# Loading and starting the next slab's norm one input block earlier, with its instructions ranked above others

## The chip, the cores and the metric

The kernel runs on one core of one Trainium2 chip. The metric is the device time of one execution in microseconds (us); lower is better. The core has a matrix engine (PE, with its weight loads as a row of their own, PEld), three engines for elementwise work (DVE, ACT, POOL), and SP, which here only issues transfers. Each engine works through its own instructions in the order in which they were written, and waits at each for the semaphores that it needs.

## The reference, cut to what matters

One inference step of a two-layer encoder, on a prompt of 2048 frames and 32 sample frames, each 1024 wide. Layer 0 mixes by sliding-window attention, layer 1 by a gated delta rule. Each layer starts with an RMS norm of its whole input; that norm is what the change moves.

```python
def rmsnorm(x, g):
    y = x * lax.rsqrt(jnp.mean(x * x, axis=-1, keepdims=True) + EPS) * g
    return y

for i in range(DEPTH):                       # DEPTH = 2
    hp = rmsnorm(xp, norm_g[i])              # prompt
    hs = rmsnorm(xs, norm_g[i])              # sample
    if i % N_MIXERS == 0:
        yp, kp, vp = attn_prompt(hp, ...)    # (softmax attention * silu(gate)) @ w_out
        ys, kd, vd = attn_sample(hs, ...)
    else:
        yp, cp, sp = deltanet_branch(hp, ...)  # conv, delta rule in chunks of 64, norm, gate, @ w_out
        ys, cd, sd = deltanet_branch(hs, ...)
    xp = xp + yp
    xs = xs + ys
y_prompt = rmsnorm(xp, final_norm_g)
y_sample = rmsnorm(xs, final_norm_g)
```

## The kernel before, in words

**Slabs and blocks.** The frames are cut into four slabs of 512 columns; slab 1 also carries the 32 sample frames and is 544 wide, worked as two groups of 272. Features lie on the 128 partitions, so a slab's input is eight tiles (k = 0 to 7). A layer's input projection goes block by block, 128 output features each: 20 input blocks a slab in the attention layer (weights `wa`), 33 in the delta layer (`wd`), then eight output blocks (`wao`, `wdo`). Every float32 operand is split into a high and a low part, and a block is 8 x 3 matmuls into the PSUM tile `pj`: 24 matmuls of 512 columns, or 48 of 272 in slab 1. The matmuls read the normalised input from tiles called `hk` (high and low part side by side) and the weights from `wh`.

**One slab's norm.** `normed` makes three steps. `start` gets the row scales and spreads them over all partitions into the tile `rb`. `ahead` loads the first three of the eight input tiles into `xa`, a ring of three buffers. `pre` starts `norm`, which for each k multiplies `xa` by `rb` and the norm's weight (DVE, scalar_tensor_tensor), casts the result into the high half of an `hk` tile (ACT), subtracts to get the low half (POOL in the attention layer, DVE in the delta layer: the argument `gcol` decides), and then loads tile k + 3 into the buffer that this frees. The input comes from `in_x` in the attention layer and from a scratch tensor (shown as `xsx`) in the delta layer.

**Buffers.** `hk` is a ring of 16. It holds a slab's eight normalised tiles and the eight tiles of the mixer's output (`og`, shown as `hk<-of` in attention and `hk<-zs` in the delta layer), which the output blocks read. A new `hk` tile takes the buffer of the one made 16 tiles earlier and can be written only when that one has been read for the last time.

**When a norm starts.** `run_blocks` walks the blocks. As a block begins it chooses the next one and calls that one's `ahead`; the block's own `pre` is called before its first matmul. The first input block of a slab carries its norm's `ahead` and `pre`. So the loads of slab n + 1 are written when slab n's last input block begins, and its norm when its own first block begins. The last input block of a slab (attention slabs, and delta slabs but the last) is marked `beside`: its matmuls are ranked as if they stood beside the block before it, so the two run interleaved. The delta layer's first slab is set apart: its norm is started from output block 2 of the last attention slab.

**Order.** Beside the blocks run generators ("sides"): the attention of a head pair, the chunks of the delta rule, the norms. They are advanced while the blocks are written down, by an estimated clock of PE. Nothing goes straight to an engine: each operation is put on a list with its dependencies and a rank,

```python
self.rank += 1
op.rank = (self.rank - self.lead, self.rank)
```

and at the end of a layer `Order.flush` plays the list through with estimated costs. Whenever an engine is free it takes, of the operations that are then ready, the one of the lowest rank. The result is the fixed order of that engine's instructions on the chip. `lead` is normally 0; evacuations of `pj` get `EVAC` = 400 and the delta rule's chain of states `CHAIN` = 600. `step`, which resumes a side, sets `lead` to 0 first. One input block at the end of a slab is some 75 to 230 operations. Some operations run far ahead of their rank, because their engine has nothing better to do.

**Which block comes next.** `pick` takes an output block of slab n if the mixer of slab n has ended on the estimated clock, and otherwise the next input block of slab n + 1 (in attention at most its first six before slab n's output blocks have all been written).

The functions that the change touches, and what calls them:

## Time and profile before

| | |
|---|---|
| three runs | 2372.67, 2376.36, 2381.98 us (median 2376.36) |
| profiled execution | 2376.4 us, its span 2374.6 us |
| mean granted TensorE clock | 0.978 |
| PE busy | 2252.8 us, 95% of the span |
| PEld, DVE, ACT, POOL busy | 1843.9, 1639.6, 1262.2, 862.9 us |
| matmuls into `pj` | 1770.1 us of PE |
| HBM traffic | 311.63 MB read, 68.19 MB written |

All instructions of this kernel carry the line of one helper (L185), so the profile is read by tile names: `pj<-hk,wh` is a projection's matmul, `xa<-xa,par,rb` the norm's multiplication, `hk<-xa` its cast, `hk<-xa,hk` its subtraction. `<-` in square brackets names what ended the idle time before an instruction. In a timeline the first number is the start in us from the beginning of the span and the second the duration.

### The profile page before, as it was taken

Reading aid. Unit: us, or ns where it says so; the run is one execution under the profiler, and the core shown is the slowest. Engines: PE = TensorE matmul, PEld = TensorE weight load, DVE = VectorE, ACT = ScalarE, POOL = GpSimd, SP = SyncE. Lnnn points to the kernel's source line nnn. Section 1 sums busy time; section 2 is a strip of 40 time slices with the busy share of each in tenths; the row PEclk is TensorE's granted clock in tenths of the full one; section 3 lists DMA queues with packets and bytes.
Section 4 is the critical chain, followed back from the end, with each engine's and each line's share of the span. In section 5 each row is a group of like instructions: output and inputs, shape, how many; then the busy total and the mean of one; then the engine's idle time right before and its main releaser. Section 6 shows DMA issues by size and latency. Waiting matters only on the chain.

```text
span 2374.6 us, 44457 instructions
## 1 busy us (share of the span) xinstructions
PE 2252.8 (95%) x14759; PEld 1843.9 (78%) x14759; DVE 1639.6 (69%) x5024; ACT 1262.2 (53%) x3792; POOL 862.9 (36%) x1044
## 2 busy tenths in 40 slices
PE   8998999999999999999999999989999999999997
PEld 5777788797778777777778788877798767777776
DVE  6765465626553445588887768889786888876876
ACT  5555466636553554455566354564644466445533
POOL 4556555665554334222322121331312222122222
PEclk9998999999999999999999999999999999999998
DMA  7556755585434115544423664333456634466442
GB/s 253 175 187 192 255 188 181 174 279 190 147 105 150 62 63 159 193 149 140 143 89 126 200 227 136 128 115 122 147 172 215 200 118 138 134 215 216 155 142 67
DMA packets 222832, 382.75 MB, mean 161 GB/s; under 512 B 29922, under 2 KB 45194, under 8 KB 222602
## 3 DMA queue, kind: packets, MB, share of 16 engines
q1 hardware_dynamic: 220154, 377.75, 49.4%
q8 instruction: 116, 1.90, 0.3%
q10 hardware_dynamic: 2448, 2.16, 0.3%
q14 instruction: 114, 0.93, 0.1%
HBM read 311.63 MB, written 68.19 MB: 160 GB/s over the span
## 4 chain that ended last, share of the span: by engine, by line
PE 56%; DVE 28%; ACT 7%; issue 4%; DMA 3%; POOL 2%; SPq 0%; DVEq 0%; ACTq 0%; POOLq 0%
PE pj L185 39%; PE tb L185 6%; PE ta L185 5%; PE tc L185 4%; DVE cy L185 4%; DVE s L185 3%; DVE sub L185 3%; DVE tl L185 3%; ACT s L185 2%; DVE ml L185 2%; ACT ta L185 1%; DVE xa L185 1%; DVE r L185 1%; DVE md L185 1%; DVE mx L185 1%
## 5 line engine op out<-in xcount | busy, mean ns | idle before, releaser
L185 PE MATMUL pj<-hk,wh 128*128 128x512 f32 (+1 forms) x8184 | 1770.1, 364 | 26.9 <-DVE xr L185 8.6
L185 PEld LDWEIGHTS pj<-hk,wh 128*128 128x128 f32 x8184 | 1326.6, 191 | 237.9 <-issue 14.1
L185 POOL TENSOR_TENSOR wh<-wr,wh 128x512 fp32r<-128x512 f32 x224 | 295.5, 1321 | 328.2 <-ACT wh L185 283.7
L185 DVE SCALAR_TENSOR_TENSOR cy<-cx,cw,cy 128x512 f32<-128x512 f32 x360 | 230.6, 651 | 44.7 <-ACT cy L185 41.1
L185 ACT CAST wh<-wr 128x512 fp32r<-128x512 f32 x224 | 138.1, 618 | 203.6 <-PE pj L185 157.3
L185 ACT ACTIVATE s<-s,mx 128x256 f32<-128x256 f32 (+1 forms) x272 | 132.0, 487 | 30.1 <-DVE mx L185 29.9
L185 ACT ACTIVATE qs<-tb,egq 64x128 f32<-64x128 f32 x264 | 95.7, 362 | 89.7 <-DVE r L185 76.5
L185 DVE TENSOR_TENSOR sub<-ml,tl 128x60 f32<-128x60 f32 (+24 forms) x527 | 125.8, 239 | 10.2
L185 DVE TENSOR_SCALAR s<-s,den 128x256 f32<-128x256 f32 (+1 forms) x272 | 130.9, 530 | 1.2
L185 ACT ACTIVATE cx<-cy 128x512 f32<-128x512 f32 (+1 forms) x96 | 61.1, 636 | 130.9 <-DVE cy L185 101.5
L185 DVE TENSOR_TENSOR tl<-tl,sub 128x60 f32<-128x60 f32 (+24 forms) x527 | 122.3, 232 | 10.1
L185 DVE CUSTOM_DVE_ANT_0 s<-ta,bias 128x256 f32<-128x256 f32 (+1 forms) x272 | 95.7, 405 | 43.5 <-PE ta L185 42.9
L185 POOL TENSOR_TENSOR pr<-pr,ph 128x512 fp32r<-128x512 f32 x82 | 111.8, 1364 | 34.9 <-ACT ph L185 28.8
L185 POOL COPY cx<-hist 128x3 f32<-128x3 f32 x96 | 25.5, 265 | 263.9 <-DVE kq L185 63.6
L185 DVE TENSOR_TENSOR xr<-pj,xr 128x512 f32<-128x512 f32 (+1 forms) x72 | 41.2, 577 | 112.1 <-PE pj L185 70.1
L185 POOL TENSOR_TENSOR so<-so,mhalf 128x4 f32<-128x4 f32 x33 | 36.8, 1115 | 216.9 <-DVE so L185 189.1
L185 DVE SCALAR_TENSOR_TENSOR r<-tb,nbk,vb 64x128 f32<-64x128 f32 x264 | 91.7, 348 | 29.6 <-PE tb L185 25.1
L185 ACT ACTIVATE qs<-o 128x128 f32<-128x128 f32 x132 | 40.7, 308 | 133.8 <-DVE o L185 128.3
L185 ACT COPY cx<-pj 128x512 f32<-128x512 f32 (+2 forms) x149 | 64.1, 445 | 77.5 <-PE pj L185 62.1
L185 PE MATMUL tb<-st,kq 128*128 128x128 f32 x512 | 94.7, 286 | 6.8 <-DVE st L185 5.9
L185 PEld LDWEIGHTS tb<-st,kq 128*128 128x128 f32 x512 | 82.9, 194 | 21.5 <-DVE st L185 13.0
L185 PE MATMUL tb<-con,s 128*128 128x128 f32 (+2 forms) x528 | 77.7, 280 | 18.9 <-DVE s L185 16.0
(242 smaller groups left out, 3558.0 us busy)
## 6 DMA issues: line engine op xcount, KB each, us to landing
wh<-xswwd SPq DMA_DIRECT2D x528, 256.0 KB
wr<-in_wa SPq DMA_DIRECT2D x160, 256.0 KB
wh<-xswwdo SPq DMA_DIRECT2D x112, 256.0 KB
pr<-in_wd SPq DMA_DIRECT2D x66, 256.0 KB
xswwd<-ph SPq DMA_DIRECT2D x66, 256.0 KB
xswwd<-pr SPq DMA_DIRECT2D x66, 256.0 KB
wr<-in_wao SPq DMA_DIRECT2D x64, 256.0 KB
xa<-in_x SPq DMA_DIRECT2D x48, 256.0 KB
```

The costliest lines, as they stand in the source:

```text
L185: self.order.add(Op(self.name, lambda: call(*args, **kw), cost, op == "dma_start"), ins, outs)
```

## The change

Two edits. In `run`, for each slab but the last of each layer, the next slab's `ahead` is called after the third last input block (index -3) and its `pre` after the second last (index -2), and both hooks are taken off the next slab's first block. So the loads and the norm's operations are each written one input block earlier, the norm's during the slab's last input block. In `norm`, `lead` is set to `EVAC` ahead of each piece of its work, so every multiplication, cast, subtraction and load of tiles 3 to 7 has a rank lower by 400. The first three loads, written by `ahead`, keep lead 0. The norm of the delta layer's first slab is called from where it was, but has the new rank too. The operations themselves, their number and shapes stay the same.

```diff
             for k in range(KT + 1):
+                self.issue.lead = Order.EVAC
                 if k < KT:
                     nc.vector.scalar_tensor_tensor(
                         out=o.x[k], in0=o.x[k], scalar=self.par[:, gcol + k : gcol + k + 1], in1=o.rb[:, :n], op0=ALU.mult, op1=ALU.mult)
                 if k:
                     yield o.x[k - 1]
                     h = self.t(self.hp, [P, 2, 544], "hk", F32R, bufs=16)
+                    self.issue.lead = Order.EVAC
                     nc.scalar.copy(h[:, 0, :n], o.x[k - 1])
                     yield
+                    self.issue.lead = Order.EVAC
                     self.low(o.x[k - 1], h[:, 0, :n], h[:, 1, :n], nc.vector if gcol else nc.gpsimd)
                     o.h.append(h)
                     if k + 2 < KT:
                         o.x.append(self.load_x(src, k + 2, slab, "xa", 3))
+                self.issue.lead = 0
...
                 out[-1].post = lambda si=si, stat=stat: (self.made.add(f"oa{si}"), self.spawn(stat(), "rstd", 1000))
+                if si + 1 < ns:
+                    self.then(blocks[-3], h1[si + 1].ahead)
+                    self.then(blocks[-2], h1[si + 1].pre)
+                    h1[si + 1].ahead = h1[si + 1].pre = None
...
                     out = self.last_outs(si, slab, og, over)
+                if si + 1 < ns:
+                    self.then(blocks[-3], h2[si + 1].ahead)
+                    self.then(blocks[-2], h2[si + 1].pre)
+                    h2[si + 1].ahead = h2[si + 1].pre = None
```

## The prediction

> **What bounds the kernel now.** I read the page's spans first, then PE's busy time in the seven stretches where one slab ends and the next begins, then PE's waits, then the timeline of two such stretches.

> ```profile
> span 2374.6 us, 44457 instructions
> PE 2252.8 (95%) x14759; PEld 1843.9 (78%) x14759; DVE 1639.6 (69%) x5024; ACT 1262.2 (53%) x3792; POOL 862.9 (36%) x1044
> ```

> PE is the bound: it is idle for 2374.6 - 2252.8 = 121.8 us in all, and no reordering can win more than that unless the clock changes. The windows show where a norm could matter (stretch, length, then busy us of PE, PEld, DVE, ACT and POOL with their instructions, then granted clock, DMA share and GB/s):

> ```profile
> 170.00:212.00 42.00, 33.65 (x201) 26.60 (x199) 33.35 (x73) 24.08 (x67) 26.36 (x22) 0.76 0.53 165
> 440.00:472.00 32.00, 27.71 (x205) 20.29 (x203) 23.42 (x65) 22.15 (x66) 24.62 (x24) 1.00 0.57 186
> 670.00:700.00 30.00, 26.26 (x182) 20.22 (x181) 22.89 (x60) 19.46 (x54) 17.03 (x16) 1.00 0.32 92
> 890.00:914.00 24.00, 21.62 (x160) 16.14 (x156) 21.33 (x56) 16.25 (x43) 9.69 (x9) 1.00 0.37 110
> 1200.00:1232.00 32.00, 28.90 (x232) 24.22 (x231) 24.23 (x87) 24.00 (x95) 12.26 (x19) 0.95 0.19 58
> 1570.00:1610.00 40.00, 31.39 (x201) 23.44 (x200) 34.44 (x111) 21.29 (x68) 15.77 (x24) 0.91 0.39 117
> 1930.00:1956.00 26.00, 22.77 (x139) 17.81 (x137) 24.44 (x66) 16.33 (x55) 11.43 (x14) 0.93 0.36 108
> sum 226.00, PE 192.32 PEld 148.72 DVE 184.10 ACT 143.56 POOL 117.16; mean PE 27.47 PEld 21.25 DVE 26.30 ACT 20.51 POOL 16.74
> ```

> The first three are the attention slabs' boundaries (call them A1, A2, A3), the fourth the step into the delta layer (X), the last three the delta slabs' (D1, D2, D3). Length minus PE busy gives idle times of 8.35, 4.29, 3.74, 2.38, 3.10, 8.61 and 3.23 us: 226.00 - 192.32 = 33.7 us, 1.4% of the span. That is what the change can reach. Only part of it is put down to the norm by name:

> ```profile
> PE tc L185 <- ACT pt L185: 6.9, 5, 4.7
> ...
> PE ta L185 <- DVE tq L185: 4.9, 9, 1.8
> PE pj L185 <- ACT hk L185: 4.8, 5, 2.1
> ...
> PE pj L185 <- DVE hk L185: 3.9, 3, 2.2
> ...
> PE pj L185 <- DMA wh<-xswwd: 3.0, 5, 0.7
> ```

> Projections wait for the norm's cast and subtraction (hk) for 4.8 + 3.9 = 8.7 us. The rest of the 33.7 are holes in the mixer's own chain, as the 4.7 us on a softmax copy (pt), which a projection that was ready could have filled.

> **The change part by part.** Nothing is added or removed. Moved are, per norm, the rows of this view:

> ```profile
> L185 DVE SCALAR_TENSOR_TENSOR xa<-xa,par,rb x80: 714/752/1920, 177.2 to 2177.1; 128x512 f32<-128x512 f32 x56, 128x544 f32<-128x544 f32 x24
> L185 SPq DMA_DIRECT2D xa<-in_x x64: 327/333/1462, 25.0 to 680.3; - x64
> L185 ACT CAST hk<-xa x56: 601/620/657, 178.0 to 1952.5; 128x512 fp32r<-128x512 f32 x40, 128x544 fp32r<-128x544 f32 x16
> ...
> L185 DVE TENSOR_TENSOR hk<-xa,hk x32: 665/684/726, 902.4 to 1953.2; 128x512 fp32r<-128x512 f32 x24, 128x544 fp32r<-128x544 f32 x8
> ...
> L185 POOL TENSOR_TENSOR hk<-xa,hk x24: 1257/1304/1837, 178.7 to 689.8; 128x512 fp32r<-128x512 f32 x16, 128x544 fp32r<-128x544 f32 x8
> ```

> Eight multiplications (8 x 0.752 = 6.0 us of DVE), eight casts (8 x 0.620 = 5.0 us of ACT), eight subtractions (10.4 us of POOL in attention, 5.5 us of DVE in the delta layer) and the loads (0.33 us of SP each, twice as many in slab 1). All of it lies beside PE's work; what reaches PE is only when the last `hk` tile is there.

> How early can that be? Writing the norm one block earlier does not by itself let it start earlier: the first three multiplications wait only for `rb` and their loads and run long ahead of their rank where DVE is free, and the first cast waits for an `hk` buffer that the last input block frees. What can shrink is the time from the first cast to the last subtraction. D2 shows it:

> ```profile
> 1575.43 1.66 ACT L185 CAST hk<-xa 128x512 fp32r<-128x512 f32 x3
> ...
> 1582.19 0.69 DVE L185 TENSOR_TENSOR hk<-xa,hk 128x512 fp32r<-128x512 f32 x1
> ...
> 1582.93 0.96 PE L185 MATMUL pj<-hk,wh 128*128 128x512 f32 x3 [1.47 <-DVE hk L185]
> ...
> 1592.23 0.51 PE L185 MATMUL pj<-hk,wh 128*128 128x512 f32 x1 [1.28 <-ACT hk L185]
> ...
> 1595.59 4.15 PE L185 MATMUL pj<-hk,wh 128*128 128x512 f32 x10 [2.19 <-DVE hk L185]
> ...
> 1605.58 0.69 DVE L185 TENSOR_TENSOR hk<-xa,hk 128x512 fp32r<-128x512 f32 x1
> 1605.60 2.80 PE L185 MATMUL pj<-hk,wh 128*128 128x512 f32 x6 [2.08 <-ACT hk L185]
> ```

> Three casts are done by 1577.1, but the first subtraction comes at 1582.2, behind the delta rule's own work on DVE; only it frees a buffer for the fourth load. In A2 a free subtraction and what follows it look like this:

> ```profile
> 442.77 1.27 POOL L185 TENSOR_TENSOR hk<-xa,hk 128x512 fp32r<-128x512 f32 x1 [2.15 <-PE tb L185]
> ...
> 446.89 1.40 DVE L185 SCALAR_TENSOR_TENSOR xa<-xa,par,rb 128x512 f32<-128x512 f32 x1 [1.54 <-DMA xa<-in_x]
> ```

> From the subtraction's end (444.04) to the next multiplication are 2.85 us. With that a round of the three buffers takes 0.69 + 2.85 + 0.75 + 0.62 = 4.9 us, and three rounds end at 1576 + 15 = 1591 instead of 1606.3. So in D2 the rank can take the norm's end forward by up to 15 us, and with it the four named waits, 1.47 + 1.28 + 2.19 + 2.08 = 7.0 us. I take **-6** (bounds 0, if DVE's other work then ends late, and -8.61, all idle). In D1 the idle time is not put down to `hk`, and half its tiles have buffers long before: **-1** of 3.10 (bounds 0 and -3.10). D3 is like D2 with a smaller hole: **-2** of 3.23 (0 and -3.23).

> In attention the norm is not alone at the end of the boundary. A1:

> ```profile
> 178.72 3.11 POOL L185 TENSOR_TENSOR hk<-xa,hk 128x544 fp32r<-128x544 f32 x2 [2.98 <-ACT hk L185]
> 178.72 1.92 DVE L185 SCALAR_TENSOR_TENSOR xa<-xa,par,rb 128x544 f32<-128x544 f32 x1
> ...
> 184.27 1.60 PE L185 MATMUL tc<-pt,vt 128*64 128x128 f32 x12 [4.68 <-ACT pt L185]
> ...
> 187.97 0.64 ACT L185 CAST hk<-xa 128x544 fp32r<-128x544 f32 x1
> ...
> 208.68 1.34 POOL L185 TENSOR_TENSOR hk<-xa,hk 128x544 fp32r<-128x544 f32 x1
> ...
> 211.28 0.73 POOL L185 TENSOR_TENSOR hk<-of,hk 128x256 fp32r<-128x256 f32 x1 [1.26 <-ACT hk L185]
> 212.54 6.72 PE L185 MATMUL pj<-hk,wh 128*128 128x272 f32 x50 [0.91 <-DVE kl L185]
> ```

> The norm ends at 210.0, the slab's attention output at 212.0. The output blocks need the latter, so they cannot start before 212; but slab 1's second block (48 of the 50 matmuls at 212.54, 6.72 x 48/50 = 6.5 us) stands behind the norm and could run before 212 if the norm ended at 200. PE has room for it: 8.35 us idle. I take **-6** (bounds 0 and -8.35). The third multiplication, done at 180.6, has its cast only at 187.97: such gaps are what the rank closes.

> In A2 and A3 both first blocks are already done when attention ends:

> ```profile
> 470.71 1.08 POOL L185 TENSOR_TENSOR hk<-of,hk 128x256 fp32r<-128x256 f32 x2
> ...
> 472.13 0.52 PE L185 MATMUL pj<-hk,wh 128*128 128x272 f32 x2 [0.25 <-DVE kl L185]
> ```

> A norm that ends sooner only moves PE's hole, unless `pick`, which then meets the first blocks earlier on its clock with the attention still running, puts a third or fourth input block ahead of the output blocks. I take half the idle times, **-2** each (bounds 0 and -4.29, -3.74).

> X has only the new rank, and there it can hurt. The output blocks wait for attention's last piece, and the norm's DVE work now goes ahead of it:

> ```profile
> 910.68 0.74 POOL L185 TENSOR_TENSOR hk<-of,hk 128x256 fp32r<-128x256 f32 x1 [2.01 <-ACT hk L185]
> ...
> 914.46 2.45 DVE L185 SCALAR_TENSOR_TENSOR xa<-xa,par,rb 128x512 f32<-128x512 f32 x2
> ```

> Two multiplications and some three subtractions run after that piece now; if all pass it, it comes 2 x 0.75 + 3 x 0.68 = 3.6 us later. I take **+2** (bounds -2.38 and +3.6).

> Queues moved past: on POOL eight subtractions of 1.30 us pass weight splits, on SP five loads pass weight loads; if the load's buffer is late on the chip, what stands behind it waits up to a round trip, 2.85 us. I cost both at nothing, since weights are loaded a block ahead (a block is 24 matmuls, some 6 us) and PE waits only 3.0 us for them in the whole span; without that cover it is up to 2.85 us at each of six boundaries, +17.

> Sum: -6 - 2 - 2 + 2 - 1 - 6 - 2 = -17. The profiled execution took 2376.4 us (1.8 beyond its span), and the median of the runs shown is 2376.36, so **2376.4 - 17 = 2359.4, say 2360 us**. A change under 0.5% (11.9 us: below 2364.5 or above 2388.3) can hardly be told from none.

> **The rivals.** *Larger gain by the clock, 2347 us.* A1 has a granted clock of 0.76, where the other attention boundaries have 1.00. If its holes close and the clock stays up, the 33.65 us of busy time shrink by up to 0.24 x 33.65 = 8 us; with all idle of A1 and D2 gone as well (another 2.35 + 2.61 = 5) it is 2360 - 13. Against it: two attention chains still alternate on a DVE that is busy for 33.35 of 42 us. [...]

> *No change, about 2371.* The mixer's chain, not the norm, ends each boundary. Then A2 and A3 give nothing, A1 and D2 some 4 and 3, X costs 2: 2376.4 - 5. For it: PE's largest waits by name are the mixer's. Against it: the four waits in D2 are the norm's alone.

> *Slower, 2391: the inversion comes late.* In D1 to D3 the norm's DVE work, 6.0 + 5.5 = 11.5 us, goes ahead of the inversion, whose result (tq) PE waits for (4.9 us, nine times). If two thirds of it lands on that chain at each, it is 3 x 7.7 = 23 us; with A1 to X at -8 that gives 2376.4 + 15. It passes +0.5% when more than (11.9 + 8) / 34.5 = 58% of that DVE work is on the path. For it: DVE is busy for 34.44 of 40 us in D2. Against it: PE has projections to fill with, and the chain of states has lead 600.

> *Slower, 2395: POOL and DVE get in each other's way.* At 178.72 a multiplication took 1.92 us beside POOL's subtraction, against 0.714 at best. If the eight subtractions, packed closer, do that to every multiplication or to a softmax step at A1 to A3, it is 3 x 8 x 1.2 = 29 us; less the 9 of D1 to D3 and a little that is paid already, about +19. It decides when over two thirds of the steps collide and DVE ends the boundary. [...]

> **How the numbers follow.** Chances: forecast 0.42, larger gain 0.15, no change 0.27, late inversion 0.10, collisions 0.06. The forecast's own range is 2349 to 2371, a fifth of it inside 0.5%. Faster: 0.34 + 0.15 + 0.01 = 0.50. Same: 0.08 + 0.22 + 0.02 = 0.32. Slower: 0.04 + 0.14 = 0.18. The range 2344 to 2386 leaves out half of the two slower rivals' chance or more and the lower tail of the larger gain, 0.2 in all; its lower end is close to 2376.4 - 33.7, all idle gone.

> **What would show it.** The cast-to-last-subtraction stretch of D2 falls from 31 us (1575.4 to 1606.3) to under 20; the waits of `pj` on `hk` fall from 8.7 us to under 4; PE idle at A1 falls from 8.35 us to under 4 with a clock above 0.85. At A2 or A3 more than 48 or 96 `pj` matmuls stand between the last input block and the first output block. The forecast is wrong if PE idle at the seven boundaries falls and the span does not: then the time went to the mixer's chain behind them, and `ta <- DVE tq` or `tb <- DVE s` will have grown. It is also wrong if the new order of all queues opens holes elsewhere, in the other 88 us of idle time, which nothing here bounds.

## The result: slower by 0.75%

The kernel after has a median of 2392.84 us in six runs (2387.80 to 2397.57), the kernel before 2373.44 us beside it. The ratio is 1.0075, with a 95% interval of 1.0059 to 1.0091. Forecast were 2360 us and a range that ended at 2386. The page of the kernel after begins:

```profile
span 2387.1 us, 44488 instructions
PE 2261.0 (95%) x14759; PEld 1849.6 (77%) x14759; DVE 1634.0 (68%) x5024; ACT 1261.7 (53%) x3792; POOL 872.7 (37%) x1044
```

The span grew by 12.5 us. PE's idle time (span less busy) grew from 121.8 to 126.1 us, its busy time by 8.2 us with the same 14759 matmuls. The mean granted clock fell from 0.978 to 0.975: two thirds of the loss are slower matmuls, one third is waiting. The seven stretches of the prediction, in the kernel after (columns as there):

```profile
170.00:212.00 42.00, 33.86 (x209) 26.38 (x208) 34.70 (x70) 25.06 (x68) 26.75 (x20) 0.88 0.49 148
440.00:472.00 32.00, 30.87 (x222) 24.66 (x222) 19.87 (x59) 19.64 (x57) 22.90 (x23) 1.00 0.57 173
670.00:700.00 30.00, 28.75 (x195) 22.03 (x193) 16.99 (x49) 16.76 (x45) 15.74 (x16) 1.00 0.29 86
890.00:914.00 24.00, 18.88 (x109) 13.97 (x108) 19.35 (x44) 14.99 (x38) 6.57 (x7) 0.93 0.29 88
1200.00:1232.00 32.00, 29.68 (x240) 25.07 (x240) 24.09 (x95) 20.89 (x87) 9.73 (x15) 0.95 0.13 43
1570.00:1610.00 40.00, 33.65 (x216) 26.05 (x215) 36.39 (x115) 24.58 (x79) 17.93 (x25) 0.90 0.44 139
1930.00:1956.00 26.00, 25.06 (x142) 19.19 (x141) 22.81 (x56) 21.16 (x75) 6.74 (x8) 1.00 0.50 153
sum 226.00, PE 200.76 PEld 157.34 DVE 174.19 ACT 143.09 POOL 106.36; mean PE 28.68 PEld 22.48 DVE 24.88 ACT 20.44 POOL 15.19
```

Idle time there fell from 33.7 to 226.00 - 200.76 = 25.2 us. Only X got worse, from 2.38 to 5.12 us; A1 hardly moved, from 8.35 to 8.14. So PE was better filled at five boundaries of seven, and the time went elsewhere. PE's waits over the whole span of the kernel after (us in total, times, longest):

```profile
PE tb L185 <- DVE s L185: 17.8, 25, 3.0
...
PE ta L185 <- DVE tq L185: 8.7, 7, 3.8
PE ta L185 <- ACT o L185: 8.6, 4, 4.2
...
PE pj L185 <- ACT hk L185: 7.1, 4, 3.6
...
PE pj L185 <- DVE hk L185: 2.9, 3, 1.6
```

and two of the same rows of the kernel before, which the prediction does not show:

```profile
PE tb L185 <- DVE s L185: 16.0, 20, 2.5
...
PE ta L185 <- ACT o L185: 3.2, 3, 2.4
```

The wait for the inversion (`tq`) grew from 4.9 to 8.7 us, that for the mixer's finished chunks (`o`) from 3.2 to 8.6. The projections' wait for `hk` did not fall: 10.0 us against 8.7. The timeline tells the norm's tiles (`hk<-xa`) from the mixer's outputs, which have the same name: the norm's part is 8.1 us against 7.4. At D2 it fell from 7.0 to 4.6, and at A1 (196.86 us) there is a new wait of 3.57 us for a cast of the norm.

To find the place I compared, block by block, when each projection block's last matmul ended in the two traces. A block is 24 or 48 `pj` matmuls, so counting them in order gives its end. The table shows how much later (+) or earlier (-) than in the kernel before the block at the same place of the order ended, in the kernel after and in kernels that are told of below (one profiled execution each). Executions differ too: up to 880 us the orders of "X only", "D1 only", "D2 only" and "D3 only" are that of the kernel before, and their first row shows -2.6 to +0.5. So a difference under some 3 us says nothing here.

| end in the kernel before, us | after | attention only | delta only | X only | D1 only | D2 only | D3 only |
|---|---|---|---|---|---|---|---|
| 800 (after A3) | -6.1 | -6.5 | +1.0 | -2.6 | +0.2 | +0.5 | +0.4 |
| 982 (after X) | -0.3 | -5.3 | +5.9 | +2.3 | +0.2 | +0.2 | +1.6 |
| 1496 (after D1) | +3.7 | -7.6 | +12.8 | +2.5 | +3.9 | -1.9 | -0.4 |
| 1675 (after D2) | -11.0 | -6.5 | -1.3 | +2.5 | +5.7 | -14.2 | -1.4 |
| 1831 | +8.6 | -7.5 | +18.3 | +2.6 | +5.0 | +5.9 | -2.7 |
| 2082 (after D3) | +13.5 | -6.3 | +23.6 | +2.1 | +5.6 | +12.6 | -5.5 |
| 2263 | +13.1 | -8.7 | +23.3 | +0.2 | +3.0 | +10.0 | +15.7 |
| 2350 (last output block 7) | +12.9 | -7.3 | +23.1 | +1.2 | +2.8 | +9.9 | +4.7 |

The kernel after wins 6 us in attention, loses them at X, runs 11 us ahead after D2, and is 8.6 us behind 150 us later.

The table counts projections alone, so a lead can also mean that other matmuls were put back. As a second measure I weighed every matmul with the median time that its shape takes in the kernel before, from its start to the next start where PE does not wait, and compared when the same sum of work was done. By this estimate the kernel after was about 3 us ahead at 1675 us, not 11: most of that lead was other work put back. It was some 4 us ahead at 1720 us and 7 to 8 behind at 1760, so it lost about 11 us within 40 us. (Other ways to weigh move the first figure by up to 3 us and the loss by 1.)

**The place behind D2.** Rows of the stretch 1700 to 1760, first before, then after (the latter also cut in pieces):

```profile
1700.00:1760.00 60.00, 58.01 (x433) 51.25 (x432) 53.87 (x181) 30.68 (x106) 14.70 (x25) 0.97 0.51 159
```

```profile
1700.00:1760.00 60.00, 52.34 (x368) 44.37 (x367) 53.37 (x188) 29.99 (x106) 14.45 (x23) 0.89 0.40 119
...
1720.00:1730.00 10.00, 4.67 (x33) 3.69 (x32) 8.92 (x47) 8.70 (x37) 4.32 (x4) 0.91 0.04 14
1730.00:1740.00 10.00, 9.56 (x77) 7.84 (x77) 8.39 (x34) 6.28 (x28) 3.89 (x10) 0.75 0.20 46
```

PE is idle for 7.66 us instead of 1.99, and the clock takes, as an estimate, 60 x (0.97 - 0.89) = 4.8 us more: 10.5 us together. The timeline says for what. Slab 1's mixer ends with the sample frames, one serial chain of four steps. Behind the last step its results get a factor (`so`: DVE, then POOL, then DVE), are scaled (ACT, `o`) and transposed (PE, `ta<-con,o`); only then can slab 1's output blocks run to their end. Before:

```profile
1710.61 6.07 PE L185 MATMUL pj<-hk,wh 128*128 128x512 f32 x25
...
1714.26 1.02 POOL L185 TENSOR_TENSOR so<-so,mhalf 128x4 f32<-128x4 f32 x1 [4.44 <-DVE so L185]
...
1715.68 1.27 ACT L185 ACTIVATE o<-o,so 128x128 f32<-128x128 f32 x4
...
1716.52 0.27 PE L185 MATMUL ta<-con,o 128*128 128x128 f32 x1
```

After:

```profile
1726.95 1.01 POOL L185 TENSOR_TENSOR so<-so,mhalf 128x4 f32<-128x4 f32 x1 [1.75 <-DVE nbk L185]
...
1728.64 1.27 ACT L185 ACTIVATE o<-o,so 128x128 f32<-128x128 f32 x4
...
1729.09 1.36 PE L185 MATMUL ta<-con,o 128*128 128x128 f32 x4 [4.24 <-ACT o L185]
```

Before, a whole input block of slab 2 (25 matmuls, 6.07 us) runs beneath that tail and PE waits for nothing. After, there is none: slab 2 may run only 15 input blocks ahead of slab 1's output blocks (`blocks[15:]` are held back until the last of those has been written), all 15 have gone, and PE stands for 4.24 us. The kernel before runs the same 15, but its last one is evacuated at 1720.6 us, behind the tail; after, at 1715.2, ahead of it. The four transposes then take 0.48 us each instead of 0.27, on the half clock (recorded from 1728.3 to 1735.1 us).

The chain itself also came 13 us later. Rows of the sample's inversion (`tq`) and of its four steps (`tb<-sst,kqs`, first to last start), before and after:

```profile
L185 PE MATMUL ta<-tq,mo x16: 218/233/234, 1662.1 to 1662.6; 32*32 32x32 f32 x16
L185 DVE STREAM_TRANSPOSE tq<-tl x1: 402/402/402, 1661.5 to 1661.5; 128x128 f32<-128x128 f32 x1
...
L185 PE MATMUL tb<-sst,kqs x16: 270/275/377, 1664.1 to 1705.6; 128*128 128x128 f32 x16
```

```profile
L185 PE MATMUL ta<-tq,mo x16: 219/233/234, 1670.4 to 1670.8; 32*32 32x32 f32 x16
L185 DVE STREAM_TRANSPOSE tq<-tl x1: 412/412/412, 1664.0 to 1664.0; 128x128 f32<-128x128 f32 x1
...
L185 PE MATMUL tb<-sst,kqs x16: 270/275/348, 1678.6 to 1719.8; 128*128 128x128 f32 x16
```

The inversion's result is there only 2.5 us later, but PE reads it 8.3 us later and begins the chain 14.5 us later: PE's fixed order now has projections of slab 2, and matmuls of other chains, in between. PE spends more of the stretch 1600 to 1700 on projections alone, first before, then after:

```profile
1600.00:1700.00 100.00, 74.39 (x259) 48.33 (x260) 0.00 (x0) 12.53 (x21) 0.95 0.39 129
```

```profile
1600.00:1700.00 100.00, 77.33 (x275) 50.10 (x274) 0.00 (x0) 13.61 (x23) 0.97 0.41 127
```

So the early norm let projections go ahead where PE was busy anyway; what they displaced was the serial chain, and they are missing where that chain has nothing else to cover it. By the second measure, the kernels told of below that have this hole lose about 11 us (delta only, D2 only) and 14 us (early only) from 1720 to 1760 us; rank only, attention only and the kernel with D2 undone lose nothing there.

### The profile page after: what moved, and what is told of

Read it like the earlier page. It is cut to its first block, busy times and chain, and to the rows that moved or that the text cites. A ratio compares the mean times of both kernels' runs of the same rounds, so it can differ in the third digit from the quotient of the medians.

```text
span 2387.1 us, 44488 instructions
## 1 busy us (share of the span) xinstructions
PE 2261.0 (95%) x14759; PEld 1849.6 (77%) x14759; DVE 1634.0 (68%) x5024; ACT 1261.7 (53%) x3792; POOL 872.7 (37%) x1044
## 4 chain that ended last, share of the span: by engine, by line
PE 58%; DVE 26%; ACT 8%; issue 4%; DMA 2%; POOL 1%; SPq 0%; DVEq 0%; ACTq 0%; POOLq 0%
PE pj L185 41%; PE tb L185 6%; PE ta L185 6%; PE tc L185 4%; DVE cy L185 4%; DVE sub L185 3%; DVE s L185 3%; DVE tl L185 3%; DVE ml L185 2%; ACT s L185 2%; ACT ta L185 1%; DVE md L185 1%; DVE r L185 1%; DVE xa L185 1%; ACT cx L185 1%
## 5 line engine op out<-in xcount | busy, mean ns | idle before, releaser
L185 PE MATMUL pj<-hk,wh 128*128 128x512 f32 (+1 forms) x8184 | 1772.8, 364 | 25.9 <-DVE xr L185 7.9
L185 PEld LDWEIGHTS pj<-hk,wh 128*128 128x128 f32 x8184 | 1331.9, 192 | 235.4 <-issue 15.9
L185 POOL TENSOR_TENSOR wh<-wr,wh 128x512 fp32r<-128x512 f32 x224 | 295.4, 1320 | 346.4 <-ACT wh L185 296.9
L185 DVE SCALAR_TENSOR_TENSOR cy<-cx,cw,cy 128x512 f32<-128x512 f32 x360 | 230.8, 651 | 42.4 <-ACT cy L185 39.4
L185 ACT CAST wh<-wr 128x512 fp32r<-128x512 f32 x224 | 137.8, 617 | 200.1 <-PE pj L185 155.7
L185 ACT ACTIVATE s<-s,mx 128x256 f32<-128x256 f32 (+1 forms) x272 | 132.0, 487 | 24.0 <-DVE mx L185 23.2
L185 ACT ACTIVATE qs<-tb,egq 64x128 f32<-64x128 f32 x264 | 95.7, 362 | 89.7 <-DVE r L185 82.7
L185 DVE TENSOR_SCALAR s<-s,den 128x256 f32<-128x256 f32 (+1 forms) x272 | 134.1, 544 | 1.3
L185 DVE TENSOR_TENSOR sub<-ml,tl 128x60 f32<-128x60 f32 (+24 forms) x527 | 125.2, 238 | 10.0
L185 ACT ACTIVATE cx<-cy 128x512 f32<-128x512 f32 (+1 forms) x96 | 61.1, 637 | 129.5 <-DVE cy L185 106.0
L185 DVE TENSOR_TENSOR tl<-tl,sub 128x60 f32<-128x60 f32 (+24 forms) x527 | 122.0, 232 | 10.3
L185 POOL COPY cx<-hist 128x3 f32<-128x3 f32 x96 | 29.0, 302 | 272.0 <-DVE sub L185 55.7
L185 DVE CUSTOM_DVE_ANT_0 s<-ta,bias 128x256 f32<-128x256 f32 (+1 forms) x272 | 96.2, 405 | 46.7 <-PE ta L185 46.2
L185 DVE TENSOR_TENSOR xr<-pj,xr 128x512 f32<-128x512 f32 (+1 forms) x72 | 41.3, 578 | 122.0 <-PE pj L185 89.8
L185 POOL TENSOR_TENSOR pr<-pr,ph 128x512 fp32r<-128x512 f32 x82 | 111.1, 1355 | 24.1 <-ACT ph L185 18.3
L185 ACT ACTIVATE qs<-o 128x128 f32<-128x128 f32 x132 | 40.8, 309 | 140.2 <-DVE o L185 130.5
L185 ACT COPY cx<-pj 128x512 f32<-128x512 f32 (+2 forms) x149 | 64.0, 446 | 95.5 <-PE pj L185 75.8
L185 DVE SCALAR_TENSOR_TENSOR r<-tb,nbk,vb 64x128 f32<-64x128 f32 x264 | 91.9, 348 | 28.1 <-PE tb L185 22.9
L185 POOL TENSOR_TENSOR so<-so,mhalf 128x4 f32<-128x4 f32 x33 | 36.7, 1112 | 197.5 <-DVE so L185 135.8
L185 POOL COPY hist<-cx 128x3 f32<-128x3 f32 x96 | 22.0, 229 | 216.3 <-ACT cx L185 215.8
L185 POOL TENSOR_TENSOR hk<-zs,hk 128x256 fp32r<-128x256 f32 x64 | 51.7, 828 | 129.8 <-ACT hk L185 129.7
L185 PE MATMUL tb<-st,kq 128*128 128x128 f32 x512 | 94.1, 287 | 5.2 <-DVE st L185 3.4
```

Source lines behind the costliest of these rows:

```text
L185: self.order.add(Op(self.name, lambda: call(*args, **kw), cost, op == "dma_start"), ins, outs)
```

## The experiments

Theory 1: the attention part is sound, and the loss has its places in the delta layer, where the mixer is made late. Theory 2: any new order deals PE's idle time anew, and no place is to blame. Theory 3 came up after the second group: what is saved or lost at one place is paid or won back further on. The expectations name them so.

**The attention layer alone.** The new rank only for the attention norms (`gcol` is 0 there), and without the second hook.

```diff
-                self.issue.lead = Order.EVAC
+                self.issue.lead = 0 if gcol else Order.EVAC
...
-                    self.then(blocks[-3], h2[si + 1].ahead)
-                    self.then(blocks[-2], h2[si + 1].pre)
-                    h2[si + 1].ahead = h2[si + 1].pre = None
```

> Both edits for the attention slabs alone; the delta layer's norms, its first one included, as before. Theory 1 (the mixer of the delta layer is made late, the attention part is sound): the 6 us gained by output block 0 of slab 2 stay and nothing is lost at the step into the delta layer, so 2367 us, ratio 0.9975. Theory 2 (every new order of the list rerolls the idle time anywhere): no relation to the parts, 0.995 to 1.008.

Measured: 2370.48 us, ratio 0.998 (0.9968 to 0.9992).

**The delta layer alone**, the mirror of it (rank only where `gcol` is not 0, hooks on `h2` only, X included).

> Both edits for the delta layer alone, the new rank for its first norm included; the attention slabs' norms as before. Theory 1: the loss at the step into the delta layer (6 us) and the 13 us lost in the delta layer stay, without the attention's 6 us: 2373 + 19 = 2392, ratio 1.008, as slow as the whole change. Theory 2: 0.995 to 1.008, and the times of this and of the attention part alone do not add up to the whole.

Measured: 2398.48 us, 1.0099 (1.0081 to 1.0117). The two parts add up: -0.20% + 0.99% = 0.79%, the whole change 0.75%. Attention gives about 5 us, the delta layer takes some 23.

**The rank alone** (both hooks left out) and **the early writing alone** (every `lead` of the norm 0), in both layers.

> The new rank in every norm, but loads and norm written where they were. Theory 1 in the form that the rank puts the norm's DVE work ahead of the mixer's: nearly all of the loss, 2386 to 2393, ratio 1.005 to 1.008. In the other form (writing the norm a block earlier, with its other places in the ring of hk and the faster estimated clock, does it): 2368 to 2376, ratio 0.998 to 1.001. Theory 2: anything from 0.995 to 1.008.

> Loads and norm written one block earlier, with the old rank. Theory 1, rank form: part of the attention's gain and no loss into the delta layer, 2366 to 2374, ratio 0.997 to 1.000. In the other form: the delta layer loses 13 as in the whole change, 2380 to 2388, ratio 1.003 to 1.006. Theory 2: anything from 0.995 to 1.008.

Measured: 2379.39 us, 1.0015 (1.0004 to 1.0027), and 2378.10 us, 1.0009 (1.0000 to 1.0018). Neither half alone is as slow as both, and 0.15% + 0.09% is not 0.75%: they work together. How was not settled. The wait behind D2 belongs to the early writing: the stretch 1700 to 1760 has 57.47 us of PE with the rank alone and 52.63 us, at a clock of 0.83, with the early writing alone. That kernel can afford it: by the second measure it was about 14 us ahead when the hole came.

**X left at its old rank**, all else as in the change.

```diff
-                self.issue.lead = Order.EVAC
+                self.issue.lead = 0 if gcol and src is self.x1[0] else Order.EVAC
```

> The change, but the delta layer's first norm (the step X from the attention layer into the delta layer) keeps its old rank. Theory 1, part X: the first norm's multiplications go ahead of the softmax work of the last attention pair, and the last output blocks of the attention layer wait; every profile with the new rank there had lost 6 to 8 us between the end of the last slab's output block 0 and its predecessor's (the change -6.1 to -0.2, delta only +0.9 to +6.8, rank only +4.7 to +11.3), the two without it 0. So about 6 us less than the changed kernel: near 2387 us, a ratio of 1.005 against the kernel before, the D2 part of the loss left. Theory 2 (any reorder deals the idle time anew): the 6 us need not stay saved through the delta layer; anywhere from 2380 to 2397 us.

Measured: 2388.58 us, 1.0062 (1.0042 to 1.0082). The median is 4 us lower than the change's, but the intervals overlap; theory 1's 1.005 lies inside. So what X costs within the whole change is not settled.

**The limit loosened** from 15 to 19 blocks.

```diff
-                self.after(f"ob{si - 1}", blocks[15:] if si else [])
+                self.after(f"ob{si - 1}", blocks[19:] if si else [])
```

> The change, with the limit on running ahead loosened: 19 instead of 15 input blocks of a delta slab may go before the output blocks of the slab before it. Theory 1, part D2 (forced output block): with the early norm, slab 2's 15 allowed input blocks are over sooner, the first output block of slab 1 comes while slab 1's mixer, whose last part is the single sample's serial chain of four steps, is still 10 to 15 us from its end, and TensorE, which takes its instructions in order, stands; that block lasted 22.9 us in the changed kernel and 7.1 us before. With four more blocks (about 33 us of products) ahead of it the wait is gone: 11 to 16 us less than the changed kernel, 2377 to 2382 us, a ratio near 1.002. Rival (the mixer itself was made late by the early norm): the four blocks then only carry the wait to another place; 2388 to 2393 us, a ratio of 1.006 or more. Theory 2: no change that can be told in the place of the wait; 2385 to 2397 us.

Measured: 2391.52 us, 1.0073 (1.0052 to 1.0095): nothing won. The windows of this kernel:

```profile
1700.00:1760.00 60.00, 56.61 (x365) 44.91 (x364) 52.38 (x167) 32.43 (x110) 20.37 (x36) 1.00 0.45 143
1880.00:2000.00 120.00, 106.15 (x642) 81.68 (x642) 99.68 (x316) 61.13 (x181) 23.77 (x41) 0.91 0.44 141
2100.00:2300.00 200.00, 188.09 (x1078) 146.43 (x1077) 154.50 (x452) 106.47 (x345) 52.94 (x83) 0.97 0.49 154
```

and of the kernel after, in the last two:

```profile
1880.00:2000.00 120.00, 111.40 (x612) 86.51 (x611) 99.14 (x304) 60.18 (x178) 27.85 (x47) 0.93 0.46 143
2100.00:2300.00 200.00, 193.41 (x1094) 151.03 (x1093) 154.70 (x459) 91.40 (x284) 53.02 (x76) 0.98 0.62 194
```

The wait at slab 1's output block 0 is gone (56.61 us of PE instead of 52.34, clock 1.00). But the next stretches lose 5.3 us of PE's time each. The cover that is spent on one chain is missing at the next: from 1880 to 2000 this kernel waits 5.9 us at once for an inversion. My claim that loosening the limit wins back what the wait at the forced output block costs is refuted.

**D2 undone**: the hooks stay at D1 and D3, all ranks stay.

```diff
-                if si + 1 < ns:
+                if si + 1 < ns and si != 1:
                     self.then(blocks[-3], h2[si + 1].ahead)
```

> The change, but at D2 alone (slab 1 to slab 2 of the delta layer) the norm keeps its old place; its rank there, and both edits at all other boundaries, stay. Theory 1, part D2: the step of 16 to 22 us at slab 1's output block 0, which the change, delta only and early only have and rank only has not, comes from this one boundary and is gone: 2375 to 2383 us, a ratio near 1.002. Rival (the early norms at D1 and D3 each cost as much): the time stays above 2388 us. Theory 2: anywhere from 2375 to 2397 us.

Measured: 2388.90 us, 1.0063 (1.0042 to 1.0085). In its profile the stretch 1700 to 1760 is whole again (56.38 us, clock 1.00), and 2100 to 2300 has 182.57 us of PE instead of 193.41. Again the loss moved.

**Put together from what had paid**: attention as in the change, in the delta layer the rank alone, without X.

> A version put together from what paid: in the attention layer both edits; in the delta layer the new rank alone, and not on its first norm (X); no early norm in the delta layer. If the parts add up: the attention part gives -5 us (2370.5 against 2374.8 us), and rank only had won back 7.5 us between the middle of the attention-to-delta step and the end (lag +11.3 to +3.8 us), so -10 to -13 us: 2362 to 2365 us, a ratio of 0.995. Rival (the 7.5 us were the recovery of a lag that this kernel hasn't got, since TensorE was behind the mixer there): no more than the attention part, 2368 to 2372 us, a ratio of 0.998. Theory 2: 2365 to 2385 us.

Measured: 2369.78 us, 0.9986 (0.9969 to 1.0003). That is the attention part and no more. It fits the rival: the 7.5 us that the rank alone had won back in the delta layer would be the recovery of a lag that this kernel has not got.

**One boundary of the delta layer at a time**, both edits there and nothing else changed from the kernel before. For D2 (X has the rank for `x1[0]` and no hook; D1 and D3 have other numbers):

```diff
+                self.issue.lead = Order.EVAC if src is self.x1[2] else 0
...
+                if si == 1:
+                    self.then(blocks[-3], h2[si + 1].ahead)
+                    self.then(blocks[-2], h2[si + 1].pre)
+                    h2[si + 1].ahead = h2[si + 1].pre = None
```

> The kernel before, with one thing alone: the new rank on the delta layer's first norm (X). Theory 1 (each boundary has a cost of its own, and they add up): 5 to 6 us more, a ratio of 1.0020 to 1.0025, since the kernels with that rank lose 5 to 7 us between the last attention slab's input blocks and its first output block. Theory 3 (the time that TensorE waits is not fixed by one boundary: what is saved or lost there is paid or won back further on, as the loosened limit and the undone D2 showed): the profile shows the 5 us at X, and less than half of it at the end; a ratio of 0.999 to 1.001.

> The kernel before, with both edits at D1 (slab 0 to slab 1 of the delta layer) alone. Theory 1: the delta-only kernel's lag grew by some 4 us between slab 0's last input blocks and slab 1's (5.9 to 9.4 us): 4 us more, a ratio of 1.0017. Theory 3: a loss or gain of a few us at D1 that changes again at the later output blocks; a ratio between 0.996 and 1.006, and the four single kernels (X, D1, D2, D3) do not add up to the 0.99% of delta only.

> The kernel before, with both edits at D2 (slab 1 to slab 2 of the delta layer) alone. Theory 1: up to 10 us ahead at slab 2's eighth input block, then the wait at slab 1's output block 0, 9 us more in sum: a ratio of 1.0038; the half-clock time between 1500 and 1800 us grows with TensorE's waits. Theory 3: the same wait at slab 1's output block 0, and a different remainder at the end, from -6 to +14 us.

> The kernel before, with both edits at D3 (slab 2 to slab 3 of the delta layer) alone. Theory 1: 4.5 us more (delta only's lag went from 19.0 to 23.3 us across it), a ratio of 1.0019, and the four single kernels add up to 0.0021 + 0.0017 + 0.0038 + 0.0019 = 0.0095, as delta only's 0.0099. Theory 3: the sum of the four is off from 0.0099 by more than 0.004.

| | median us | ratio | 95% interval |
|---|---|---|---|
| X | 2383.12 | 1.0036 | 1.0022 to 1.0050 |
| D1 | 2380.82 | 1.0023 | 1.0009 to 1.0037 |
| D2 | 2386.73 | 1.0050 | 1.0036 to 1.0063 |
| D3 | 2384.69 | 1.0038 | 1.0026 to 1.0050 |

Each boundary costs by itself: four new orders, four losses, no interval with 1.000 in it. That speaks against theory 2, but does not rule it out: a fair coin gives four losses once in 16. And the four make 1.47% where delta only has 0.99%. So theory 1's sum is off as well, by 0.48 points, where theory 3 asked for more than 0.4; the spread of the runs leaves that difference uncertain by some 0.4 points (my estimate), so it barely tells the two apart. The sums come right if D3's 0.38% is left out wherever D2 is in place: 1.09% for delta only (0.99), 0.89% for the whole change (0.75), 0.53% without X (0.62), and with D3 counted 0.77% without D2 (0.63). Each lies inside its run's interval. That rule was found from these runs, and not tested by others.

D1 loses just behind its boundary. By the second measure D1 alone loses 4 to 6 us from 1200 to 1350 us, where D2 alone and D3 alone lose nothing. From 1234 to 1345 us PE's named waits add up to 6.7 us instead of 3.5, in many small ones; the largest sum is for a convolution's copy (`cy`, 2.5 us in four).

X shows its cost where it was looked for. The waits and the stretch of that kernel:

```profile
PE tb L185 <- DVE s L185: 3.5, 2, 3.0
```

```profile
880.00:920.00 40.00, 34.05 (x214) 25.61 (x213) 30.97 (x85) 24.23 (x66) 11.73 (x11) 0.96 0.30 94
```

The kernel before has 37.30 us of PE there, clock 1.00 and no wait on `s`. The norm's multiplications and subtractions stand ahead of the softmax (`s`) of the last attention pair; the table shows the lag go from -2.6 to +2.3, 4.9 us, and stay there until 2082. (The profiled execution was the fastest of its six, 2375.28 us, so it shows where, and the median how much.)

D2 alone has the change's hole with the change's numbers: 52.05 us of PE from 1700 to 1760 at 0.89, and these two waits (the second from the stretch 1880 to 2000):

```profile
PE ta L185 <- ACT o L185: 4.2, 1, 4.2
...
PE ta L185 <- DVE tq L185: 3.8, 1, 3.8
```

D3 alone loses far behind D3. From 2100 to 2300 it has

```profile
2100.00:2300.00 200.00, 182.99 (x1046) 139.42 (x1045) 152.56 (x455) 103.31 (x334) 55.73 (x82) 0.98 0.52 165
```

where D2 alone has 192.76 and the kernel before 193.03. It takes 12 input blocks of slab 3 ahead of slab 2's output blocks instead of 13, is 14 us ahead of the kernel before at 2178 us, and 15.7 behind at 2263 (some 10 by the second measure). Its largest waits there are for weight loads (4.4 us in three), for the chain's state (`st`, 3.8 us in four) and for a convolution's result (`vf`, 2.7 us). Why D2 takes this away was not settled.

## Why the prediction was wrong

- **A1 to A3, -10 forecast: right direction, half the size.** Attention only measures -0.20% (4.7 us; -1.9 to -7.6), and the lag after A3 is -6. At A2 and A3 idle time fell from 8.0 to 2.4 us. At A1 it stayed (8.35 to 8.14): the 4.68 us hole is gone, and the wait of 3.57 us for the norm's cast came in its place. The clock there went from 0.76 to 0.88, but part of that is chance: in six kernels with the attention part of before it was 0.76 to 0.85, in six with that of after 0.84 to 0.92. No further input block was put ahead of the output blocks; both boundaries ended sooner, with two as before.
- **X, +2: sign right, size wrong.** X alone costs 0.36%, 8.5 us (5.2 to 11.9); its trace shows 4.9 us at the place. The bound of 3.6 us counted the operations that run after attention's last piece and could pass it. The ones that hurt pass the softmax of the pair before that.
- **D2, -6 (0 to -8.61): the step that failed most.** The prediction put all 8.7 us of waits on `hk` down to the norm; 7.4 were its own, 7.0 of them at D2. The norm did become shorter, though less than thought. Its casts and subtractions in the kernel after:

```profile
L185 ACT CAST hk<-xa x8: 601/618/626, 1579.1 to 1601.1; 128x512 fp32r<-128x512 f32 x8
L185 DVE TENSOR_TENSOR hk<-xa,hk x8: 671/688/1097, 1580.6 to 1602.9; 128x512 fp32r<-128x512 f32 x8
```

  They take 24.5 us from the first cast to the end of the last subtraction, instead of 31; under 20 was forecast. Idle time at D2 fell from 8.61 to 6.35 us, and the projections ran 11 us ahead. The gain itself came near its forecast: by the second measure D2 alone wins about 4 us from 1560 to 1720 us. Then it loses about 11 us by 1760 and 6 more between 1880 and 1960. D2 alone costs 0.50%, 11.9 us. The upper bound of 0 was wrong: it let DVE's other work end late, but held that a hole of PE, once filled, stays filled. The matmuls that fill it are the same that later lie beneath the mixer's serial chains; they were taken from there.
- **D1 -1 and D3 -2** have the wrong sign: +0.23% and +0.38%. D1 loses just behind its boundary, in many small waits, so the bound of 0 failed there too. D3 loses far behind its boundary, and its cause stays open.
- **Weight loads, put at nothing:** right for the change, where PE's waits on them fell from 3.0 to 0.9 us.
- **The clock** was weighed only for a gain at A1. Some of it came, and the mean over the span still fell, from 0.978 to 0.975: behind the new holes of 4.2 and 3.8 us the clock was half for 6.8 and 10.2 us. In this trace the recorded clock changes only on steps of 3.41 us, and the steps just ahead of these two drops, at 1728.3 and 1909.2 us, were wholly idle.
- **The rival "the inversion comes late"** (2391 us) had the time and the direction, and its cause only in part. It put the norm's DVE work on the inversion's path. The wait on `tq` did grow, by 3.8 us, but at D2 the sample's inversion ended only 2.5 us later; the larger delay was made by PE's own order, 8.3 us until it read the result. The collisions of POOL and DVE were not tested on their own, but the trace speaks against them: the 24 multiplications at A1 to A3 took 26.8 us in sum instead of 24.6, the 24 subtractions on POOL 33.7 instead of 33.1, and that part of the change won time.
- **The sign named in advance** is what came: idle time at the boundaries fell by 8.4 us, the span grew, and `ta <- DVE tq` and `tb <- DVE s` grew, with `ta <- ACT o`, which I had not named, growing most.

No version beat the kernel before by 0.5%. The attention part alone is the best, at 0.998.

## What to carry to other kernels

Where one engine is full and takes its instructions in a fixed order, independent matmuls are a stock of cover: before work is moved ahead to fill a hole, ask which later chain the same work covers now, and price the hole that it leaves there. Here the limit on running ahead showed where the shortage would appear, and moving the limit only moved it. Measure each place of a change that acts at many places by itself; here one half paid and the other cost five times as much.
